# The second norm's gain folded into router, shared and gathered weights in a hybrid decoder layer, and expert pairs released from the shared expert

## The chip, the cores and the metric

The kernel runs on one core of one Trainium2 chip. The metric is the device time of one execution in microseconds. It was run three times; the profiled execution is a further one.

## The reference, cut to what matters

One decoder layer over 512 tokens of width 1024: a mixer (attention and a short convolution), a sandwich of norms, then a mixture of 32 experts with top-1 group and top-2 experts per token, and a shared expert.

```python
h = h + rms_norm(mix, post_mix_norm)
t = rms_norm(h, pre_ffn_norm)                  # x * rsqrt(mean(x*x) + eps) * g   <- g is the gain per feature
logits = t @ w_group_router, t @ w_expert_router
combine = top-1 group, top-2 experts of the group, softmax weights
hid = silu(t @ w_gate[e]) * (t @ w_up[e]) * combine[:, e]
routed = sum over e of hid @ w_down[e]
shared = (silu(t @ w_sh_gate) * (t @ w_sh_up)) @ w_sh_down
h = h + rms_norm(routed + shared, post_ffn_norm)
```

The gain `g` (`pre_ffn_norm`, in the kernel `g_ffn`) is applied per feature. Every use of `t` is a matrix product over features, so the gain can stand in the tokens or in the rows of the weights.

## The kernel before, in words

A Python generator scheduler writes the program out: generators yield conditions, `run` (line 267) picks the one with the lowest priority number that the planner `Progress` (lines 62 to 146) thinks can go on, and its instructions go to the engines' queues in that order. The order of each queue is thus fixed when the program is written; on the chip an engine only waits.

Memory for weights and for large tiles is 25 slots of about 1 MB (`NSLOT`, `slot`, `rel`, `take`, `reserve`, `pump`, lines 181 to 231). `Slots` counts free slots while the program is written. `rel` hands slots back and `pump` at once puts the next queued weight loads on SP's queue, one per free slot; slots asked for with `reserve` go first. Which of the 25 places a tile gets is not decided there: it is given its place when the program's first write to it is reached, and that write waits for the last use of what was there.

The weight loads stand in `Slots.queue` in a fixed order (lines 394 to 406): shared gate and up `(32, 0)` and `(32, 1)`; then 16 pairs of experts, six loads of 1 MB each, named `(expert, part)` with parts 0 and 1 for gate and up and 2 for down: pair 0 is experts 0 and 16, pair 1 is 17 and 1, pair 2 is 2 and 18, pair 3 is 19 and 3; `(32, 2)`, the shared down weight, stands behind pair 2; at the end `gp`, and the rows of `y_d` and `h_d` for the last sum (`kk`, `hb`).

The stages around the change, for four chunks `c` of 128 tokens:

- `out_split_gen` (945) loads the two gains into tile `gb`: `g_mix` in its first half and `g_ffn`, copied to all partitions, in its second.
- `attn_out_gen` (1003) makes the mixer's output; behind its last chunk `take` (1024) hands back six slots and takes `rs` (tables of the router), `xg` (gathered rows) and `hs` (shared hidden values).
- `chain_gen` (1029) does the first norm's sum, stores `h_d`, and makes `t` in tile `x` (`tt(c)`) by one VectorE instruction with the scale per token and the gain (1043).
- `router_gen` (1046) transposes `t` (`ptT`), copies it to `tT`, stores `t_d`, and makes the logits from the router weights `wrt` (in tile `m1`).
- `shared_gen` (1084) makes gate and up of the shared expert in matmuls `psh`, 64 records a chunk, at the lowest priority; after the last chunk and with the routing done (flag `idx`) it sets `gu` and hands back both shared weights and both `tT` tiles (1103).
- `route` (1135) makes the token lists per pair in `rs` on VectorE, ends in `idx`, `wgt`, `cnt`, issues the first two gathers of rows from `t_d`, starts `pairs_gen`, and goes on with `overflow_tables` (1334), which reads and writes `rs` to its last instruction and then hands `rs` back (1283).
- `pairs_gen` (1459) reserves `wk` and `yb`, waits for `gu`, transposes the gathered rows (`xpose`, `pxt`, into `wk`) and then does each pair: gate and up (`pgu`, four steps for part 0, four for part 1), `hidden`, down (`pdn`), a scatter to `y_d`. The two weights of a part are handed back behind it.
- `last_gen` (1549) sums routed and shared parts and writes the output.

Of the kernel before, what the change touches and what calls it, by code (L numbers as in the profile page):

```python
# [18 lines left out]
P = 128  # L19
# [146 lines left out]
def hymba_kernel(ctx: ExitStack, tc: tile.TileContext, xT, xmT, x, meta, cpk, pos, wqkv, wconv, wuq, wukv,  # L166
# [43 lines left out]
    def keep(n):  # L210
        Slots.keep = n
        pump()
# [96 lines left out]
    def every(*needs):  # L309
        return lambda: max(f() for f in needs)  # L310
# [68 lines left out]
    queue_load("conv0", wconv[0], ok=lambda: True)  # L379
    pump()  # L380
    Y.dma_start(mt[:NMETA, :D], meta)
    Y.dma_start(posi, pos)
    for q in range(2):
        Y.dma_start(xs[1][:, q * D:(q + 1) * D], x[(2 + q) * P:(3 + q) * P, :])
# [129 lines left out]
    for k in range(8):  # L514
        mm3(pqm[:NMETA, :160], [xmhl[:, a, k, :] for a in range(2)], [wqk(k, a)[:, 256:416] for a in range(2)],
            k == 0, k == 7)


    ssc = cp.tile([P, NT], F32, name="ssc")
# [391 lines left out]
    def finish(c):  # L911
        ac, pmT, mg = A["ac"], A["m"], A["mg"]
        yield every(at(ac), free_bank(2))
        pb = bank("prb")
        for i in range(4):
            tr(pb[:, i * P:(i + 1) * P], ac[:, i * P:(i + 1) * P])
        S.activation(ac, pb, AF.Copy)
        pb = bank("pmT")
        tr(pb[:, :P], SMs[:, c].rearrange("p h m -> p (h m)"))
        V.tensor_copy(pmT, pb[:, :P])  # L920
        yield at(pmT)
        for i in range(4):
            mm(OUTP[c][:, i * P:(i + 1) * P], vm[:, i * P:(i + 1) * P], pmT, start=False, stop=True,
               skip_group_check=True)
        V.tensor_tensor(ac, OUTP[c], ac, op=OP.mult)
        o = slice(c * 512, (c + 1) * 512)
        S.activation(mg[0][:, o], ac, AF.Copy)
        V.tensor_tensor(mg[1][:, o], ac, mg[0].bitcast(F32)[:, o], op=OP.subtract)
        S.activation(ac, ac, AF.Square)
        V.tensor_reduce(pmT, ac.rearrange("p (i n) -> p n i", i=4), axis=AX.X, op=OP.add)  # L930
        spawn(attn_out_gen(c, [m[:, o] for m in mg]), 4)
        yield every(at(pmT), free_bank())
        ps = bank("pas")
        mm(ps[:, :1], pmT, ones, start=True, stop=True)
        rstd(sst[:, c, 0:1], ps[:, :1], 1.0 / 512)
        cv["fin", c] = True
        if c == NT - 1:
            rel(A["b"])
            Y.dma_start(wrt, wr)


    wo = {}
# [2 lines left out]
    def out_split_gen():  # L945
        for k in (4, 5, 6, 7, 0, 1, 2, 3):
            n = f"out{k // 2}"
            yield every(loaded(n), room(1 if k % 4 else K_WO), idle("ACT", "DVE", early=W_IDLE))
            o = G_AO + k if k < 4 else G_CO + k - 4
            wo[k] = split_half(Slots.have[n], k % 2, "wo", ck[:, o:o + 1])  # L950
            if k % 2:
                rel(got(n))
        yield room(2)
        late["gb"], late["x0"] = slot("gb"), slot("x0")
        Y.dma_start(late["gb"][:, :D], g_mix[None, :].to_broadcast([P, D]))
        Y.dma_start(late["gb"][:, D:2 * D], g_ffn[None, :].to_broadcast([P, D]))
        for c in range(2):
            Y.dma_start(tt(c), x[c * P:(c + 1) * P, :])
        yield room(1)
        late["x1"] = slot("x1")  # L960
        for c in range(2, NT):
            Y.dma_start(tt(c), x[c * P:(c + 1) * P, :])
        keep(0)

    def mix(c):
        return mixs[c // 2][:, (c % 2) * D:(c % 2 + 1) * D]
# [36 lines left out]
    def attn_out_gen(c, mg):  # L1003
        yield every(flag(wo, *range(4)), flag(cv, ("co", c)), flag(late, f"x{c // 2}"))
        if c:
            yield flag(cv, ("done", c - 1))
        yield at(*mg, *(wo[k] for k in range(4)))
        ss = small([P, 4], "ss", bufs=4)
        m = mix(c)
        for half in range(2):  # L1010
            yield free_bank()
            ps = bank("pao")
            for k in range(4):
                mm3(ps, [mg[a][:, k * P:(k + 1) * P] for a in range(2)],
                    [wo[k][:, b * 1024 + half * 512:b * 1024 + (half + 1) * 512] for b in range(2)], k == 0, k == 3)
                yield
            yield flag(cv, ("fin", c))
            o = slice(half * 512, (half + 1) * 512)
            V.scalar_tensor_tensor(m[:, o], ps, sst[:, c, 0:1], m[:, o], op0=OP.mult, op1=OP.add)
            S.activation(junk[:, :512], m[:, o], AF.Square, accum_out=ss[:, half:half + 1])  # L1020
            (V if c + half >= G_POOL else G).tensor_tensor(m[:, o], m[:, o], late["gb"][:, o], op=OP.mult)
        cv["done", c] = True
        if c == NT - 1:
            rt["rs"], rt["xg"], sh["hs"] = take(["rs", "xg", "hs"], *(wo[k] for k in range(4)), *A["mg"])
            rt["place"] = rt["rs"][:, 1792:1920]
            S.activation(rt["place"], slotc, AF.Copy)
        spawn(chain_gen(c, ss), 0 if c == NT - 1 else 1)

    def chain_gen(c, ss):
        gb, m = late["gb"], mix(c)  # L1030
        yield at(ss)
        V.tensor_tensor(ss[:, 2:3], ss[:, 0:1], ss[:, 1:2], op=OP.add)
        rstd(sst[:, c, 1:2], ss[:, 2:3], 1.0 / D)
        yield at(sst[:, c, 1:2], m)
        V.scalar_tensor_tensor(m, m, sst[:, c, 1:2], tt(c), op0=OP.mult, op1=OP.add)
        S.activation(junk, m, AF.Square, accum_out=ss[:, 3:4])
        S.dma_start(h_d[c * P:(c + 1) * P, :], m)
        yield at(ss[:, 3:4])
        rstd(sst[:, c, 2:3], ss[:, 3:4], 1.0 / D)
        if c == NT - 1:  # L1040
            G.memset(rt["xg"], 0.0)
        yield at(sst[:, c, 2:3])
        V.scalar_tensor_tensor(tt(c), m, sst[:, c, 2:3], gb[:, D:2 * D], op0=OP.mult, op1=OP.mult)
        spawn(router_gen(c), 0 if c == NT - 1 else P_ROUTER)

    def router_gen(c):
# [10 lines left out]
        if "lg" not in rt:  # L1057
            yield free_bank()
            rt["lg"] = bank("plg")
            held.append(rt["lg"])  # L1060
        yield every(at(*(tT(k, c * P, (c + 1) * P) for k in (0, 4))), free_bank())
        ps = bank("plT")
        for k in range(0, 8, 2):
            for q in range(2):
# [16 lines left out]
    def acc(c):  # L1081
        return sh["out"][c // 2][:, (c % 2) * D:(c % 2 + 1) * D]

    def shared_gen():
        yield loaded((NE, 0), (NE, 1))
        w = [got((NE, i)) for i in range(2)]
        for c in range(NT):
            yield flag(cv, ("tT", c))
            yield every(at(*w, *(tT(k, c * P, (c + 1) * P) for k in (0, 4))), free_bank(2))
            ps = bank("psh")  # L1090
            for g in range(4):
                for k in range(8):
                    o = (k % 4) * 512 + (g % 2) * 256 + (g // 2) * P
                    mm(ps[:, g * P:(g + 1) * P], w[k // 4][:, o:o + P], tT(k, c * P, (c + 1) * P),
                       start=(k == 0), stop=(k == 7))
                    yield
            yield flag(sh, "hs")
            hs_ = sh["hs"]
            S.activation(hs_[:, c * 512:(c + 1) * 512], ps, AF.Copy)
        yield flag(cv, *(("lg", c) for c in range(NT)))  # L1100
        yield flag(rt, "idx")
        sh["gu"] = True
        rel(*w, *tTs)
        yield flag(sh, "silu")
        hs = hs_[:, :2048].rearrange("p (c f g n) -> p c f g n", c=NT, f=2, g=2)
# [184 lines left out]
                             bounds_check=SEQ - 1, oob_is_err=False)  # L1290

    def xpose(src, dst, by=S):
        for q in range(2):
            ps = bank("pxt")
            for k in range(4):
                tr(ps[:, k * P:(k + 1) * P], src[:, (4 * q + k) * P:(4 * q + k + 1) * P])
            if q and by is V:
                V.tensor_copy(dst[:, q * 512:(q + 1) * 512], ps)
            else:
                S.activation(dst[:, q * 512:(q + 1) * 512], ps, AF.Copy)  # L1300

    def hidden(ps, w, sg, hd):
        S.activation(sg, ps[:, :256], AF.Silu)
# [153 lines left out]
            Y.dma_start(out[c * P:(c + 1) * P, :], h)  # L1457

    def pairs_gen():
        box = reserve("wk", "yb")  # L1460
        ys = None
        yield flag(sh, "gu")
        yield lambda: 0.0 if box else INF
        wk_, yb = box
        rt["wk"] = wk_
        rt["jk"] = wk_.bitcast(BF)[:, 3584:3584 + 512]
        xt_ = wk_[:, :D]
        sg, hd, ht = (wk_[:, D + q * 256:D + (q + 1) * 256] for q in range(3))
# [4 lines left out]
        for j, es in enumerate(pairs):  # L1473
            ps = None
            for i in range(2):
                yield every(loaded(*((e, i) for e in es)), free_bank())
                w = [got((e, i)) for e in es]
                yield at(*w, xt_)
                if ps is None:
                    ps = bank("pgu")  # L1480
                for k in range(4):
                    col2(ps, xt_[:, (4 * i + k) * P:(4 * i + k + 1) * P],
                         [w[q][:, k * 512:(k + 1) * 512] for q in range(2)], i + k == 0, i + k == 4)
                rel(*w)
            hidden(ps, wgt[:, j:j + 1], sg, hd)
            sh["silu"] = True
            if j == S_GO:
# [134 lines left out]
    spawn(conv_gen(), 6)  # L1622
    spawn(conv_out_gen(), 3)
    spawn(route(), P_ROUTE)
    spawn(shared_gen(), 8)
    run()
    overflow()
# [81 lines left out]
```

## Time and profile before

| | us |
|---|---|
| median of 3 runs | 508.37 |
| lowest, highest | 507.75, 508.88 |
| profiled execution, its own time | 507.05 |
| span from the first to the last instruction | 505.3 |
| TensorE busy | 479.0 (95%) |
| VectorE, ScalarE, GpSimd busy | 227.0, 163.4, 87.3 |
| moved by DMA | 151.30 MB, mean 299 GB/s |

All positions are microseconds from the span's start; 1.75 us lie outside of the span. The engines are named PE (TensorE), DVE (VectorE), ACT (ScalarE), POOL (GpSimd) and SP (the queue that issues most transfers). A busy PE is not PE at its peak, since the shares are averages over stages with different limits, and matmul ends are modelled.

### The profile page before, as it was taken

The numbers are of one execution on the slowest core, as the hardware profiler recorded it, in microseconds if no ns is written. First come the engines' busy times: TensorE is split into PE (matmuls) and PEld (weight loads), VectorE is DVE, ScalarE is ACT, GpSimd is POOL, SyncE is SP. The second block draws the span as 40 slices with busy tenths as digits, with TensorE's granted clock in tenths as the row PEclk, the third lists the DMA queues.
The fourth block names the chain that finished last, engine by engine and source line by source line (L and its number), as shares of the span: only waits on it lengthen the run. The fifth ranks groups of instructions, "written<-read, shape, count | busy, mean of one in ns | idle before, by whom it ended". The sixth has DMA issues, their size and how long they took to land. (4 is left out here: it accounts for less than half of the span.)

```text
span 505.3 us, 7279 instructions
## 1 busy us (share of the span) xinstructions
PE 479.0 (95%) x2780; PEld 303.0 (60%) x2780; DVE 227.0 (45%) x522; ACT 163.4 (32%) x334; POOL 87.3 (17%) x114
## 2 busy tenths in 40 slices
PE   8999999999999999997999999999999999988893
PEld 7998999788767788897963333433333333223251
DVE  6478789656877642678832111001111111111175
ACT  5775526445345642532122112211111111111131
POOL 2034234400000002460101111001111111100011
PEclk9999999999999999999999999999999999999997
DMA  8962240090207598399659999999999999999993
GB/s 291 401 248 83 84 167 0 35 382 2 84 2 279 220 354 325 134 382 381 242 239 421 417 423 420 422 416 421 420 420 419 420 420 417 420 419 424 405 365 150
DMA packets 30309, 151.30 MB, mean 299 GB/s; under 512 B 5480, under 2 KB 5864, under 8 KB 16192
## 3 DMA queue, kind: packets, MB, share of 16 engines
q1 hardware_dynamic: 24512, 138.43, 68.1%
q0 software_dynamic: 4464, 8.17, 4.4%
q10 hardware_dynamic: 1296, 4.21, 2.1%
q8 instruction: 23, 0.38, 0.3%
q14 instruction: 14, 0.11, 0.1%
HBM read 140.54 MB, written 18.35 MB: 314 GB/s over the span
## 5 line engine op out<-in xcount | busy, mean ns | idle before, releaser
L314 PE MATMUL pc<-xh,cw 128*128 128x256 f32 (+2 forms) x320 | 70.0, 309 | 0.0
L159 DVE SCALAR_TENSOR_TENSOR wk<-wk,wgt,pgu 128x256 f32<-128x256 f32 x16 | 7.7, 480 | 115.3 <-ACT wk L159 115.3
L314 PEld LDWEIGHTS pc<-xh,cw 128*128 128x128 f32 x320 | 52.3, 189 | 4.0 <-issue 1.3
L159 ACT ACTIVATE wk<-pgu 128x256 f32<-128x256 f32 x16 | 6.1, 383 | 133.7 <-PE pgu L314 133.7
L314 PE MATMUL pc<-xl,cw 128*128 128x256 f32 (+2 forms) x160 | 48.8, 305 | 0.0
L159 DVE COPY yb<-pdn 128x512 f32<-128x512 f32 x15 | 10.4, 692 | 60.4 <-PE pdn L314 60.4
L159 POOL DMA_INDIRECT xg<-t_d,idx x16 | 16.5, 1030 | 114.3 <-PE pxt L314 68.8
L159 POOL DMA_INDIRECT y_d<-yb,sidx x15 | 15.1, 1005 | 93.2 <-DVE yb L159 81.9
L314 PEld LDWEIGHTS pc<-xl,cw 128*128 128x128 f32 x160 | 30.4, 190 | 1.2
L159 ACT ACTIVATE att<-pS,nm 128x128 f32<-128x128 f32 (+3 forms) x32 | 16.9, 527 | 29.3 <-DVE nm L159 27.2
L314 PE MATMUL pS<-kT,qT 128*128 128x128 f32 (+3 forms) x64 | 22.7, 440 | 0.0
L159 POOL TENSOR_TENSOR sst<-rst,neghalf 128x1 f32<-128x1 f32 x12 | 7.5, 633 | 81.5 <-DVE rst L159 78.1
L314 PEld LDWEIGHTS pxt<-ident,xg 128*128 128x128 f32 x128 | 14.0, 140 | 11.3 <-issue 9.7
L314 PE MATMUL pco<-wo,cvh 128*128 128x512 f32 x64 | 20.6, 403 | 0.0
L314 PE MATMUL pao<-wo,mgh 128*128 128x512 f32 x64 | 20.0, 393 | 0.0
L159 POOL TENSOR_TENSOR cw<-ld conv,cw 128x1024 fp32r<-128x1024 f32 x6 | 15.7, 2618 | 18.5 <-ACT cw L159 18.5
L159 ACT ACTIVATE yb<-pdn 128x512 f32<-128x512 f32 x15 | 9.0, 597 | 29.2 <-PE pdn L314 29.2
L314 PE MATMUL psh<-tT,ld (32, 1)_1946 128*128 128x128 f32 x128 | 18.0, 279 | 0.0
L314 PE MATMUL psh<-tT,ld (32, 0)_1944 128*128 128x128 f32 x128 | 17.8, 279 | 0.0
L314 PE MATMUL pxt<-ident,xg 128*128 128x128 f32 x128 | 17.3, 278 | 0.0
L159 DVE TENSOR_REDUCE nm<-pS 128x1 f32<-128x128 f32 (+3 forms) x32 | 15.5, 484 | 1.7 <-PE pS L314 1.4
L314 PEld LDWEIGHTS psh<-tT,ld (32, 1)_1946 128*128 128x128 f32 x128 | 15.9, 192 | 0.2 <-issue 0.2
(486 smaller groups left out, 1190.5 us busy)
## 6 DMA issues: line engine op xcount, KB each, us to landing
ld conv<-in_wconv_dram SPq DMA_DIRECT2D x6, 1024.0 KB
ld out<-in_wout_dram SPq DMA_DIRECT2D x4, 1024.0 KB, 4.7
y_d<-sel SPq DMA_DIRECT2D x4, 1024.0 KB
ld kk<-y_d SPq DMA_DIRECT2D x4, 1024.0 KB
xs<-in_x_dram SPq DMA_DIRECT2D x4, 512.0 KB
x<-in_x_dram SPq DMA_DIRECT2D x4, 512.0 KB
h_d<-mix ACTq DMA_DIRECT2D x4, 512.0 KB
t_d<-x ACTq DMA_DIRECT2D x4, 512.0 KB, 10.2
```

The lines of the kernel that those rows point to most:

```text
L159: r = f(*a, **k)
L314: f(o, *ins, **kw)
```

## The change

The gain `g_ffn` is no longer multiplied into `t`. It is loaded as a small tile, transposed once into `gf` (128 x 8: one column per block of 128 features), and multiplied into the router weights (one VectorE instruction), into the shared gate and up weights (eight ScalarE instructions in a new generator of priority 1), and into the gathered rows as they are copied out of PSUM. `t` itself is made by a ScalarE copy with the scale per token. `pairs_gen` no longer waits for `gu`: `wk` is taken with `rs`, `xg` and `hs`, and `yb` is reserved behind the first half of pair 0. `hs` is written early by a small memset.

```diff
+    gfr = mt[:8, 1536:1536 + P]
+    Y.dma_start(gfr, g_ffn.rearrange("(k p) -> k p", k=8))
...
+    gf = cp.tile([P, 8], F32, name="gf")
+    tr(pqm[:, 480:488], gfr, ident[:8, :8])
+    V.tensor_copy(gf, pqm[:, 480:488])
...
@@ out_split_gen
-        Y.dma_start(late["gb"][:, D:2 * D], g_ffn[None, :].to_broadcast([P, D]))
...
         keep(0)
+        yield flag(cv, "wrt")
+        yield at(wrt)
+        w3 = wrt.rearrange("p (k n) -> p k n", k=8)
+        V.tensor_tensor(w3, w3, gf[:, :, None].to_broadcast([P, 8, 64]), op=OP.mult)
+        cv["wrg"] = True
...
@@ attn_out_gen, behind the last chunk
-            rt["rs"], rt["xg"], sh["hs"] = take(["rs", "xg", "hs"], *(wo[k] for k in range(4)), *A["mg"])
+            rt["rs"], rt["xg"], rt["wk"], sh["hs"] = take(["rs", "xg", "wk", "hs"],
+                                                          *(wo[k] for k in range(4)), *A["mg"])
+            G.memset(sh["hs"][:, 0:1], 0.0)
...
@@ chain_gen
-        V.scalar_tensor_tensor(tt(c), m, sst[:, c, 2:3], gb[:, D:2 * D], op0=OP.mult, op1=OP.mult)
+        S.activation(tt(c), m, AF.Copy, scale=sst[:, c, 2:3])
...
@@ router_gen
-        yield every(at(*(tT(k, c * P, (c + 1) * P) for k in (0, 4))), free_bank())
+        yield every(flag(cv, "wrg"), at(*(tT(k, c * P, (c + 1) * P) for k in (0, 4))), free_bank())
...
-    def shared_gen():
+    def shared_scale_gen():
         yield loaded((NE, 0), (NE, 1))
         w = [got((NE, i)) for i in range(2)]
+        for k in range(8):
+            yield every(at(w[k // 4]), idle("ACT", early=1.0))
+            o = w[k // 4][:, (k % 4) * 512:(k % 4 + 1) * 512]
+            S.activation(o, o, AF.Copy, scale=gf[:, k:k + 1])
+        sh["w"] = w
+
+    def shared_gen():
+        yield flag(sh, "w")
+        w = sh["w"]
...
         yield flag(cv, *(("lg", c) for c in range(NT)))
-        yield flag(rt, "idx")
-        sh["gu"] = True
         rel(*w, *tTs)
...
@@ xpose
-            if q and by is V:
-                V.tensor_copy(dst[:, q * 512:(q + 1) * 512], ps)
+            if by is V:
+                V.tensor_tensor(dst[:, q * 512:(q + 1) * 512].rearrange("p (k n) -> p k n", k=4),
+                                ps.rearrange("p (k n) -> p k n", k=4),
+                                gf[:, 4 * q:4 * q + 4, None].to_broadcast([P, 4, P]), op=OP.mult)
             else:
-                S.activation(dst[:, q * 512:(q + 1) * 512], ps, AF.Copy)
+                for k in range(4):
+                    S.activation(dst[:, q * 512 + k * P:q * 512 + (k + 1) * P], ps[:, k * P:(k + 1) * P], AF.Copy,
+                                 scale=gf[:, 4 * q + k:4 * q + k + 1])
...
@@ pairs_gen
-        box = reserve("wk", "yb")
-        ys = None
-        yield flag(sh, "gu")
-        yield lambda: 0.0 if box else INF
-        wk_, yb = box
-        rt["wk"] = wk_
+        wk_, yb, ys, box = rt["wk"], None, None, None
...
+                if j + i == 0:
+                    box = reserve("yb")
                 rel(*w)
+            if j == 0:
+                yield lambda: 0.0 if box else INF
+                yb = box[0]
...
+    spawn(shared_scale_gen(), 1)
```

## Rows read from the trace of the kernel before

**Rows 1.** The page's second part: GB/s in 40 equal slices of 12.6 us.

```profile
GB/s 291 401 248 83 84 167 0 35 382 2 84 2 279 220 354 325 134 382 381 242 239 421 417 423 420 422 416 421 420 420 419 420 420 417 420 419 424 405 365 150
```

**Rows 2.** Stretches: us, busy of PE, PEld, DVE, ACT, POOL, clock, DMA share, GB/s.

```profile
160.00:210.00 50.00, 50.00 (x286) 39.55 (x285) 24.55 (x42) 22.63 (x43) 9.57 (x10) 1.00 0.69 269
...
246.00:257.00 11.00, 10.94 (x110) 10.77 (x110) 9.73 (x44) 0.60 (x1) 1.58 (x2) 1.00 0.22 61
257.00:262.00 5.00, 4.69 (x29) 2.38 (x30) 0.89 (x6) 2.87 (x4) 0.99 (x1) 1.00 0.84 329
262.00:300.00 38.00, 35.75 (x176) 13.15 (x174) 6.88 (x11) 6.81 (x14) 6.07 (x6) 1.00 1.01 419
300.00:340.00 40.00, 40.00 (x166) 15.43 (x163) 3.73 (x7) 8.28 (x16) 4.05 (x4) 1.00 1.02 420
340.00:470.00 130.00, 120.80 (x570) 44.96 (x568) 18.64 (x30) 19.72 (x40) 18.15 (x18) 1.00 1.02 420
```

**Rows 3.** Timeline of SP's queue: start us, us, engine line op out<-in.

```profile
237.12 0.44 SPq L159 DMA_DIRECT2D ld (18, 2)_2418<-in_we_dram  x1
256.68 0.33 SPq L159 DMA_DIRECT2D ld (32, 2)_2605<-in_we_dram  x1
...
257.90 0.33 SPq L159 DMA_DIRECT2D ld (3, 0)_2654<-in_we_dram  x1
258.33 0.53 SPq L159 DMA_DIRECT2D ld (19, 1)_2680<-in_we_dram  x1
262.40 0.33 SPq L159 DMA_DIRECT2D ld (3, 1)_2682<-in_we_dram  x1
...
272.13 0.33 SPq L159 DMA_DIRECT2D ld (4, 0)_2733<-in_we_dram  x1
```

**Rows 4.** Waits of SP's queue: waited for, us in total, times, longest.

```profile
SPq L159 <- PE psh L314: 19.0, 1, 19.0
...
SPq L159 <- DVE code L159: 0.3, 1, 0.3
```

**Rows 5.** Timeline of PE around the start of the pairs; brackets: idle before, releaser.

```profile
231.13 1.06 PE L314 MATMUL ptT<-ident,x 128*128 128x128 f32 x8 [2.75 <-DVE rs L159]
...
256.49 1.06 PE L314 MATMUL psh<-tT,ld (32, 1)_1946 128*128 128x128 f32 x8
257.38 1.04 PE L314 MATMUL pxt<-ident,xg 128*128 128x128 f32 x8
258.73 0.64 PE L314 MATMUL pgu<-ld (0, 0)_1948,wk 128*64 128x512 f32 x1 [0.31 <-ACT wk L159]
...
271.51 0.59 PE L314 MATMUL pdn<-ld (0, 2)_1972,wk 128*64 128x512 f32 x1
```

**Rows 6.** Timeline of ACT in the same stretch.

```profile
217.48 0.29 ACT L159 ACTIVATE rs<-m 128x128 f32<-128x128 f32 x1
...
224.31 1.06 ACT L159 ACTIVATE m<-mix 128x1024 bf16<-128x1024 f32 x1 [0.88 <-DVE rst L159]
...
231.10 0.60 ACT L159 ACTIVATE hs<-psh 128x512 f32<-128x512 f32 x1 [5.64 <-DMA t_d<-x]
...
258.07 1.09 ACT L159 ACTIVATE wk<-pxt 128x512 f32<-128x512 f32 x2
```

**Rows 7.** Timeline of DVE in the same stretch.

```profile
229.71 1.28 DVE L159 SCALAR_TENSOR_TENSOR x<-mix,sst,gb 128x1024 f32<-128x1024 f32 x1
...
244.23 0.17 DVE L159 SCALAR_TENSOR_TENSOR idx<-ptb,rs 128x16 int32<-128x16 f32 x1
...
257.65 0.17 DVE L159 TENSOR_TENSOR code<-code,rs 128x8 f32<-128x8 f32 x1
```

**Rows 8.** Timeline of POOL: the first gather.

```profile
245.29 1.29 POOL L159 DMA_INDIRECT xg<-t_d,idx  x1 [17.92 <-DVE rs L159]
```

**Rows 9.** Instructions of tile xg: time from issue to landing of its gathers.

```profile
DMA to landing us min/median/max: 7.9/8.1/9.3
```

**Rows 10.** Transfers from 244 to 252 us: GB/s in 40 slices of 0.2 us.

```profile
GB/s 369 532 369 369 492 328 451 287 246 82 0 82 82 0 41 41 143 246 123 205 287 225 164 205 143 246 144 185 184 246 144 123 41 0 0 0 0 0 0 0
```

More of the change, by code (lines that the diff above doesn't have):

```diff
@@ L939, in finish @@
             Y.dma_start(wrt, wr)
+            cv["wrt"] = True
     wo = {}
@@ L1029, in chain_gen @@
     def chain_gen(c, ss):
-        gb, m = late["gb"], mix(c)
+        m = mix(c)
         yield at(ss)
```

## The prediction

> **What bounds the kernel now.** I read the page's slices first. From slice 21 on, that is from 265 us, DMA moves about 420 GB/s without a break until the last 25 us [rows 1]. PE is shown busy nearly all the time as well, but the stretches tell which of the two is short: from 340 to 470 us PE idles 9.2 of 130 us while DMA stays at 420 GB/s, and from 262 to 340 DMA is as full while PE catches up [rows 2]. So from 258 us on the kernel streams weights, and its end stands where the stream's start and its holes put it. A microsecond in which DMA idles before 258 us costs one at the end; a microsecond of PE does not, unless it makes such a hole.
>
> The hole that the change can touch is the stretch from 246 to 257 us: 61 GB/s [rows 2]. SP's queue shows why: load (18, 2), the last of pair 2, is issued at 237.12, the next one, (32, 2), at 256.68 [rows 3], after a wait of 19.0 us for the shared matmuls psh [rows 4]. All 25 slots are full then: rs, xg, hs, two tT, two shared weights and 18 loads, pairs 0 to 2. At 256.49 to 257.55 PE ends psh, then transposes for pair 0 and starts its gate and up at 258.73 [rows 5]. Four loads go out from 256.68 to 258.33 [rows 3]. From 257 to 262 us 329 GB/s pass, 1.65 MB, which is 3.9 us at 420, so the stream stands as if it had started at 258.1, 1.4 us behind the first issue [rows 2, 3].
>
> **How memory is handed out.** Three rows show that a tile's place is fixed at its first write, and waits for what last used it there. hs is taken with the slots of the mixer's weights (line 1024), but its first ScalarE write idles 5.64 us for a store t_d<-x, a reader of a token tile [rows 6]. Load (3, 0) waits 0.3 us for the VectorE tile code [rows 4] and is issued at 257.90; the last instruction that reads rs for code starts at 257.65 and takes 0.17 [rows 3, 7]: it lies where rs lay. Load (19, 1) goes out at 258.33, before any weight of pair 0 is done, though five slots came back and wk and yb had reserved two of them [rows 3]: a reservation holds no memory.
>
> **The change, part by part.**
>
> *The wait of the pairs.* Without the flag, pair 0 can start when its rows are gathered and wk has a place. wk is now taken at line 1024, one load fewer is counted there, but wk is first written by the copies of pair 0. The hand-back of rs (line 1283) comes in the program before that: route goes on at once, while the planner lets a gather land 1.2 + 1.5 + 0.9 + 2.0 us after its issue (lines 135 to 139). So (18, 2) is queued by rs's hand-back, finds the spare place free, and the same 18 loads are in before the hole. wk then gets the place of rs, which is free when overflow_tables is done. My main step is this: **the pairs wait for the router's tables instead of for shared.** It needs no new instruction; the copies on ScalarE wait, PE stands behind them in its queue, and the shared matmuls that are left then stand behind PE's wait.
>
> *How much earlier the tables are.* idx is made at 244.23, the last read of rs ends at 257.82, 13.6 us later [rows 7]; this chain is unchanged. What comes earlier is idx. PE waits 2.75 us, to 231.13, for the last chunk's t [rows 5], which VectorE makes at 229.71 in 1.28 us between router instructions [rows 7]; the memset gives hs an early place, so the 5.64 us on ScalarE go too [rows 6]. Both stalls overlap. I take 2.75 us, the one that the chain shows; bounds are 0 (the next release is late by as much) and 5.64. The tables then end at 255.07.
>
> *The ScalarE copy that makes t.* A ScalarE pass over 128 x 1024 takes 1.06 us [rows 6], the VectorE form 1.28 [rows 7]; the move buys 0.2 us and a place outside VectorE's queue, and is in the 2.75. The Trainium skill, ScalarE: Activation LUTs, section Rules for kernel authors, says the opposite of a multiply: use VectorE, up to about three times faster per element in bf16. Taken at that factor, an estimate from that page, the copy would cost some 2.6 us more, the 2.75 would be gone, and the sum below would come to 515.3. The rows are float32 and decide.
>
> *Pair 0's copies.* Two of 128 x 512, 1.09 us together [rows 6], become eight of 128 x 128, 0.29 each [rows 6]; PE follows piece by piece, so 0.5 us pass to its first matmul: 255.07 + 0.5 = 255.6. It was 258.73.
>
> *What the stream makes of that.* Before, it did not wait for pair 0: four slots came back from shared. Now its first free slots are pair 0's own. From PE's first matmul to the issue into the first weight's place it is 262.40 - 258.73 = 3.67 us [rows 3, 5], so (32, 2) and (19, 0) go out at 259.3, and the stream starts 1.4 later, at 260.7: **2.6 us later than 258.1.** One more load, (3, 0), follows after the second half; the fourth place goes to yb. Three loads of 1.05 MB at 420 GB/s are 7.5 us, to 268.2. The next two come when pair 0's down is done, (272.13 - 258.73) = 13.4 us behind its start [rows 3, 5]: 269.0, flowing at 270.4. That is a hole of 2.2 us. One gather of 0.31 MB (half of what passes from 247 to 250.6 us [rows 10]) fills 0.7 of it: **1.5 us**, between 0 and 2.2. Behind that a pair's six loads take 15 us of DMA and PE does a pair in 13.4, so the stream stays fed.
>
> *The rest, at no cost.* The shared weights' scaling is eight passes of about 0.6 us, 4.8 us, on ScalarE from 160 to 210 us, where it is busy 22.6 of 50 [rows 2] and PE is fed by other work; without that cover it costs up to 4.8. The router weights' product (128 x 512, about 0.7 us) falls into the same stretch of VectorE, 24.6 of 50 [rows 2]. The gain's small load and its transpose come in the first 30 us; they cost 0 to 0.5 us of PE's order. The load of g_ffn that goes is 0.5 MB, 1.2 us of a DMA that is not full there. In pairs 1 to 15 VectorE makes both halves of a copy; VectorE is busy 18.6 of 130 us [rows 2], and DMA covers it. These edits together: 0, from -1 to +1.
>
> *Sum.* 2.6 + 1.5 = 4.1 us later. The rows are of an execution of 507.05 us (span 505.3), 1.3 below the median of 508.37; on the median it is 508.4 + 4.1 = **512.5**. The kernel would be as fast as before if pair 0 started at 251.5.
>
> **Rivals.**
>
> *A: wk has a place at once, and the pairs start with their rows; faster.* Its place is in the router's last 13.6 us: it decides if a slot other than rs's is free for wk, or rs is. Then the gather sets the start: issued at 245.29 - 2.75 = 242.5 [rows 8]. The first two gathers' data ended at 250.6, 5.3 us behind the issue, with DMA otherwise empty [rows 10]; that gives 247.9, and pair 0 at 249.2 (1.35 from pxt to pgu [rows 5]): 2.3 us under the mark, **506.1**. With the landing of 7.9 to 9.3 us that gathers show in the stream [rows 9] it is 251.8, or 508.7. For it: line 1024 takes wk while six places are free. Against it: nothing writes wk then, and hs shows what that leads to [rows 6].
>
> *B: the lead is larger.* With 5.64 us, pair 0 starts at 252.7 and the time is 509.6; only 6.9 would make it even. So "no change" mostly needs part of A.
>
> *C: shared keeps four slots too long; slower still.* Its two weights and two tT now wait for gaps of PE. From 300 to 340 us PE has no idle time at all [rows 2], with a stream that is just fed. Four loads are 10 us; if they are missing there for long, up to that much is lost: 516 to 522. Against it: the same PE work is done by then, and a pair still frees places faster than DMA fills them.
>
> **How the numbers follow.** About 0.2%, 1 us, is what a measurement of this kernel can tell from no change. The main case has 0.53 and gives 509.6 (B's lead) to 515.3 (no lead); C has 0.1. A has 0.3: two thirds of it below 507.4, the rest near even. 0.07 is for small edits that give or take a microsecond. Faster 0.22, same 0.15, slower 0.63. The range takes in A's low end and the main case's high one: 505.9 to 515.5; the main case's own is 509.6 to 515.3.
>
> **What would show it.** Right: in the timeline of ScalarE the first wk copy idles for VectorE's code or rs; PE idles for several us before pgu of pair 0, which starts near 255.6; SP's wait for psh is replaced by one for pgu that ends near 259; the hole in GB/s lasts to about 260.7, with a dent near 269; hs no longer waits for t_d, and idx is made near 241.5. Wrong: pgu of pair 0 before 251.5, with a wk copy that waits for pxt alone (A); dents in GB/s between 270 and 340 us (C); or idx no earlier than 244, which would mean that the stall of 2.75 us only moved.

## The result and the profile after

The changed kernel takes **526.58 us** (median of 4 runs, 525.95 to 527.36), the kernel before in the same session 508.62: a ratio of 1.0347 (95% interval 1.032 to 1.0373). The forecast was 512.5, within 505.9 to 515.5. The direction was right; the size was far off. The profiled execution spans 525.6 us, against 505.3 before: 20.3 us to account for.

Two places hold all of it, and both show in the page's slices, which answer to [rows 1] (slices of 13.1 us). The clock that was granted to PE falls twice, in the third slice and in the twenty-first. In the twenty-first slice GB/s falls to 25, and the next one, from 276 us, has 338; before, the slice from 265 us on already had 421.

```profile
PEclk9978999999999999999979999999999999999998
DMA  8941124064203877499608999999999999999993
GB/s 303 401 197 62 34 75 154 2 225 176 81 2 122 319 281 297 168 350 405 249 25 338 414 422 420 422 419 422 418 424 418 419 420 421 419 421 422 401 377 132
```

**Before 60 us: VectorE waits for a copy.** The timeline of VectorE of the changed kernel, then that of ScalarE, then that of PE (start, duration, engine, line, operation, tiles, and in brackets the idle time before and what ended it):

```profile
16.74 0.29 DVE L159 TENSOR_TENSOR kvs<-mt,kvs 128x128 fp32r<-128x128 f32 x1
26.20 0.17 DVE L159 COPY gf<-pqm 128x8 f32<-128x8 f32 x1 [9.17 <-PE pqm L314]
26.32 0.07 DVE L159 MEMSET ssx<- 128x16 f32 x1
29.73 1.23 DVE L159 TENSOR_TENSOR cw<-ld conv,cw 128x1024 fp32r<-128x1024 f32 x1 [3.34 <-ACT cw L159]
```

```profile
26.43 1.06 ACT L159 ACTIVATE m<-xs 128x1024 bf16<-128x1024 f32 x1 [11.02 <-DVE ssx L159]
...
28.66 1.04 ACT L159 ACTIVATE cw<-ld conv 128x1024 fp32r<-128x1024 f32 x1
```

```profile
25.94 0.22 PE L314 MATMUL pqm<-ident,mt 8*128 8x8 f32 x1
29.75 0.58 PE L314 MATMUL pc<-xh,cw 128*128 128x256 f32 x1 [3.59 <-ACT cw L159]
...
42.00 0.39 PE L314 MATMUL pc<-xh,cw 128*128 128x258 f32 x1 [2.01 <-DVE ctmp L159]
```

The gain's transpose stands on PE behind all projections and starts at 25.94. Its copy to gf stands on VectorE ahead of the memset of ssx, so VectorE does nothing for 9.17 us. ScalarE's sums of squares wait for ssx, and the split of the first convolution weights is queued behind them. Before, these ran while PE was still projecting; the same three engines then read:

```profile
21.22 1.23 DVE L159 TENSOR_TENSOR cw<-ld conv,cw 128x1024 fp32r<-128x1024 f32 x1 [3.93 <-ACT cw L159]
```

```profile
17.32 1.06 ACT L159 ACTIVATE m<-xs 128x1024 bf16<-128x1024 f32 x1 [1.69 <-DVE ssx L159]
```

```profile
26.05 0.32 PE L314 MATMUL pc<-xh,cw 128*128 128x256 f32 x1
```

The windows of the changed kernel give the price (us, busy time and count of PE, PEld, DVE, ACT, POOL, then the granted clock, DMA share, GB/s):

```profile
20.00:30.00 10.00, 6.41 (x49) 6.05 (x48) 0.46 (x3) 3.54 (x6) 0.00 (x0) 0.95 1.03 420
30.00:40.00 10.00, 9.53 (x56) 8.86 (x56) 5.30 (x9) 9.68 (x28) 1.20 (x1) 0.71 0.24 101
40.00:50.00 10.00, 8.00 (x50) 7.82 (x51) 6.89 (x24) 3.36 (x6) 4.19 (x2) 0.83 0.01 3
```

PE is busy 23.94 of these 30 us (30.00 before): 6.06 us are idle time. In its busy time it lacks 5, 29 and 17% of its clock, 0.3 + 2.8 + 1.4 = 4.5 us. Together that is 10.5 us, and that is by how much the load of g_mix is late: 161.45, before 150.97. The split into idle time and clock is read from the windows alone; no run separates the two here.

**From 230 us on: the mechanism that was forecast, with other numbers.** The timelines of VectorE, ScalarE and PE, and SP's queue, which answer to [rows 3, 5, 6, 7]:

```profile
255.09 0.17 DVE L159 SCALAR_TENSOR_TENSOR idx<-ptb,rs 128x16 int32<-128x16 f32 x1
...
268.51 0.17 DVE L159 TENSOR_TENSOR code<-code,rs 128x8 f32<-128x8 f32 x1
```

```profile
238.21 1.15 ACT L159 ACTIVATE x<-mix,sst 128x1024 f32<-128x1024 f32 x1 [2.46 <-POOL sst L159]
...
268.79 2.17 ACT L159 ACTIVATE wk<-pxt,gf 128x128 f32<-128x128 f32 x8 [9.65 <-DVE code L159]
```

```profile
269.21 1.12 PE L314 MATMUL pgu<-ld (0, 0)_1951,wk 128*64 128x512 f32 x1 [4.40 <-ACT wk L159]
...
270.12 1.06 PE L314 MATMUL pgu<-ld (0, 0)_1951,wk 128*64 128x512 f32 x1
...
275.00 0.59 PE L314 MATMUL pgu<-ld (0, 0)_1951,wk 128*64 128x512 f32 x1
```

```profile
250.44 0.42 SPq L159 DMA_DIRECT2D ld (18, 2)_2628<-in_we_dram  x1
275.62 0.33 SPq L159 DMA_DIRECT2D ld (32, 2)_2681<-in_we_dram  x1
...
279.06 0.33 SPq L159 DMA_DIRECT2D ld (3, 0)_2693<-in_we_dram  x1
285.22 0.33 SPq L159 DMA_DIRECT2D ld (19, 1)_2734<-in_we_dram  x1
```

wk lies where rs lay: its first copies wait 9.65 us for the end of the tables, and PE behind them. pgu of pair 0 starts at 269.21, which is 258.73 and the 10.5 us from the front: the pairs start no earlier at all. Then SP issues (32, 2), 6.41 us behind pgu. The windows, answering to [rows 2]:

```profile
267.50:272.00 4.50, 2.79 (x8) 0.94 (x10) 1.21 (x8) 3.19 (x9) 0.00 (x0) 0.55 0.00 1
272.00:275.50 3.50, 3.50 (x14) 0.99 (x12) 0.00 (x0) 0.26 (x1) 0.00 (x0) 0.61 0.00 0
275.50:280.00 4.50, 4.50 (x27) 1.95 (x24) 0.48 (x2) 0.39 (x1) 0.00 (x0) 1.00 0.72 271
280.00:285.00 5.00, 5.00 (x31) 2.62 (x31) 1.20 (x3) 0.98 (x2) 0.99 (x1) 1.00 0.99 418
285.00:290.00 5.00, 5.00 (x26) 1.72 (x24) 0.69 (x1) 0.00 (x0) 1.01 (x1) 1.00 0.88 293
```

After its 4.40 us without work PE is granted 0.55 and 0.61 of its clock, mostly the lower of its two levels (1.2 of 2.4 GHz), and a matmul of pair 0 takes 1.06 us instead of 0.59. The last window is the forecast dent: 293 instead of 420 GB/s over 5 us, 1.5 us. From 300 us on DMA moves 420 GB/s as before.

So the theory that the experiments were to test was this: 8 to 10 us come from the place of one copy, the rest from pair 0, which starts no earlier, at half the clock, and feeds the stream from its own places.

### The profile page after: what moved, and what is told of

Its sections match the earlier page's. It is cut to its first block, busy times and chain, and to the rows that moved or that the text cites. A ratio compares the mean times of both kernels' runs of the same rounds, so it can differ in the third digit from the quotient of the medians.

```text
span 525.6 us, 7292 instructions
## 1 busy us (share of the span) xinstructions
PE 488.8 (93%) x2781; PEld 307.5 (58%) x2781; DVE 231.1 (44%) x536; ACT 165.2 (31%) x337; POOL 83.1 (16%) x114
## 5 line engine op out<-in xcount | busy, mean ns | idle before, releaser
L314 PE MATMUL pc<-xh,cw 128*128 128x256 f32 (+2 forms) x320 | 73.9, 320 | 6.1 <-ACT cw L159 3.6
L314 PEld LDWEIGHTS pc<-xh,cw 128*128 128x128 f32 x320 | 55.4, 201 | 10.7 <-ACT cw L159 3.7
L314 PE MATMUL pc<-xl,cw 128*128 128x256 f32 (+2 forms) x160 | 50.6, 316 | 0.0
L314 PEld LDWEIGHTS pc<-xl,cw 128*128 128x128 f32 x160 | 32.2, 201 | 1.2
L159 DVE TENSOR_TENSOR wk<-pxt,gf 128x512 f32<-128x512 f32 x30 | 19.2, 683 | 10.0 <-PE pxt L314 10.0
L314 PE MATMUL psh<-tT,ld (32, 0)_1947 128*128 128x128 f32 x128 | 18.4, 280 | 0.0
L314 PE MATMUL psh<-tT,ld (32, 1)_1949 128*128 128x128 f32 x128 | 18.4, 278 | 0.0
L314 PEld LDWEIGHTS psh<-tT,ld (32, 1)_1949 128*128 128x128 f32 x128 | 16.1, 192 | 0.2 <-issue 0.2
## 6 DMA issues: line engine op xcount, KB each, us to landing
xs<-in_x_dram SPq DMA_DIRECT2D x4, 512.0 KB, 8.8
x<-in_x_dram SPq DMA_DIRECT2D x4, 512.0 KB
h_d<-mix ACTq DMA_DIRECT2D x4, 512.0 KB
t_d<-x ACTq DMA_DIRECT2D x4, 512.0 KB, 7.3
```

The costliest lines, as they stand in the source:

```text
L159: r = f(*a, **k)
L314: f(o, *ins, **kw)
```

## The experiments

All times are medians; the kernel before, run beside each, was at 508.1 to 509.2. Every kernel from e1 on contains the edit of e1, except e2.

| run | what | us | ratio to before (95%) |
|---|---|---|---|
| after | the change | 526.58 | 1.0347 (1.0320 to 1.0373) |
| e1 | gain's copy later | 518.38 | 1.0190 (1.0161 to 1.0219) |
| e2 | before, with the gain's copy alone | 516.98 | 1.0172 (1.0138 to 1.0205) |
| e4 | e1, PE kept busy 8.2 us | 520.30 | 1.0232 (1.0202 to 1.0263) |
| e8 | e1, PE kept busy 4.2 us | 517.01 | 1.0156 (1.0138 to 1.0173) |
| e3 | e1, wk with a place of its own | 513.42 | 1.0097 (1.0066 to 1.0128) |
| e5 | e1, last x ahead of the router | 517.43 | 1.0162 (1.0141 to 1.0183) |
| e10 | e5, PE's order as well | 517.43 | 1.0181 (1.0151 to 1.0211) |
| e11 | e10 and e8 | 516.14 | 1.0157 (1.0123 to 1.0191) |
| e13 | e10, shared held back | 515.67 | 1.0135 (1.0094 to 1.0175) |
| e12 | e13 and e8 | 514.24 | 1.0114 (1.0073 to 1.0154) |
| e7 | e1, pairs wait for shared | 509.81 | 1.0011 (1.0001 to 1.0021) |
| e9 | e7, last x ahead of the router | 508.05 | 0.9985 (0.9971 to 0.9998) |

**e1: the copy moved.**

```
-    gf = cp.tile([P, 8], F32, name="gf")
-    tr(pqm[:, 480:488], gfr, ident[:8, :8])
-    V.tensor_copy(gf, pqm[:, 480:488])
...
     conv_split(1)
+    gf = cp.tile([P, 8], F32, name="gf")
+    tr(pqm[:, 480:488], gfr, ident[:8, :8])
+    V.tensor_copy(gf, pqm[:, 480:488])
```

> The changed kernel, with the gain's transpose and its copy to gf moved behind the second split of the convolution weights; nothing else. My theory: 10.5 us of the loss arise before 60 us, because the copy to gf stands on VectorE ahead of the memset of ssx and waits there for PE to come through all its projections (it idles 9.17 us, to 26.20; in the kernel before, the memset ran at 17.22). Behind it ScalarE idles 11.02 us, PE 3.59 and 2.01 us, and the granted clock falls to 0.71. With the copy moved those waits go, the load of g_mix is back near 151 us (161.45 in the changed kernel), and the time is 526.6 - 10.5 = 516.1 (515.0 to 517.5). Rival: the gain's own load, its transpose and the longer hold of mt cost the time wherever they stand; then the time stays at 524 or more.

518.38, 8.2 us less; the range asked for 515.0 to 517.5, so the theory holds for four fifths of its 10.5. VectorE's timeline of e1 has the memset at 17.38 (before 17.22), and the copy waits for nothing; the lines of PE and of SP's queue are from the start of the pairs.

```profile
17.38 0.07 DVE L159 MEMSET ssx<- 128x16 f32 x1
...
28.05 0.16 DVE L159 COPY gf<-pqm 128x8 f32<-128x8 f32 x1
```

```profile
260.87 1.11 PE L314 MATMUL pgu<-ld (0, 0)_1951,wk 128*64 128x512 f32 x1 [4.40 <-ACT wk L159]
```

```profile
266.93 0.33 SPq L159 DMA_DIRECT2D ld (32, 2)_2681<-in_we_dram  x1
```

From 20 to 50 us the clock is 1.00, and PE idles 0.9 us. The load of g_mix goes out at 152.95, 8.5 us earlier, but not near 151 as expected; where the other 2.0 us stay is not shown. pgu of pair 0 is at 260.87 instead of 269.21, 8.3 us earlier, and still 2.1 us later than before; the last mix is 0.9 us late (223.86, before 222.94), the rest arises in the router (below).

**e2: the same instructions, alone, in the kernel before.**

```
+    gfr = mt[:8, 1536:1536 + P]
+    Y.dma_start(gfr, g_ffn.rearrange("(k p) -> k p", k=8))
...
+    gf = cp.tile([P, 8], F32, name="gf")
+    tr(pqm[:, 480:488], gfr, ident[:8, :8])
+    V.tensor_copy(gf, pqm[:, 480:488])
```

> The kernel before, with nothing added but the gain's load into mt, its transpose and its copy to gf, at the places where the changed kernel has them; nobody reads gf. My theory: the whole early loss comes with these three instructions, so the time is 508.6 + 10.5 = 519.1 (518 to 520.5), with VectorE's copy idle near 9 us and the clock near 0.7 between 30 and 40 us. Rival: the early loss needs other parts of the change (other orders of loads or of splits that the planner makes of it); then it stays within 1 us of 508.6.

516.98: 7.8 us slower than the kernel before, a microsecond under the range, and the copy reads as it does in the changed kernel. The clock fell less than expected, to 0.83 from 30 to 40 us, and was 1.00 behind that; PE idled 7.0 us between 20 and 50. Three instructions that move 4 KB make some 8 of the 18 us of the loss; put elsewhere (e1) or put in alone (e2), they are worth the same.

```profile
26.57 0.17 DVE L159 COPY gf<-pqm 128x8 f32<-128x8 f32 x1 [9.08 <-PE pqm L314]
26.69 0.07 DVE L159 MEMSET ssx<- 128x16 f32 x1
```

**e4 and e8: the clock.** PE is given work in its wait; the bank is overwritten by the first real matmul.

```
                 if ps is None:
                     ps = bank("pgu")
+                    for q in range(36 if j == 0 else 0):     # e8: 18
+                        T.matmul(ps[:, :P], ident, ident, start=True, stop=True)
```

> As e1, and PE is kept at work in its wait for pair 0's rows: 36 matmuls of 128 x 128 float32, of the kind and speed of psh (8 in 0.9 us, so 4.0 us in all), write into the bank of pgu before its first real matmul overwrites it. In the changed kernel PE idles 4.40 us there, the granted clock reads 0.55 to 0.61 from 267.5 to 275.5, and the first half of pair 0 takes 6.2 us instead of 3.5. My theory: that clock costs 2.7 us, so the time is 2.7 us under that of e1: 513.4 (512.8 to 514.2). Rival: the stream's start does not hang on PE's speed there, or the clock falls for another reason; then it is the same as e1 within 0.7 us.

520.30, which is 1.9 us more than e1 and outside both ranges: my sizing was wrong. A float32 matmul of this kind counts twice in the rows (x72 for 36), so the 36 took 8.21 us and pushed pgu to 264.44. Behind them the clock read 1.00. So e8 took half.

> As e4_fill with 18 matmuls instead of 36. In e4_fill the 36 took 8.21 us (each counts twice), not 4.0, so they ended 3.6 us after pair 0 could have started; yet behind them the clock read 1.00 and the first half of pair 0 took 3.5 us instead of the 5.9 of e1_gain_later. My theory: 18 of them take 4.1 us and end within the wait, pgu starts at 260.9 as in e1_gain_later, its first half takes 3.5 us, and the time is 2.4 us under e1_gain_later's 518.4: 516.0 (515.2 to 516.7). Rival: the stream's start does not hang on the clock: 518.4 within 0.7.

517.01, 1.4 us less than e1: outside both ranges, and less than the 2.4 expected. PE's timeline of e8 and SP's queue of e8:

```profile
256.39 4.18 PE L1502 MATMUL pgu<-ident 128*128 128x128 f32 x36
260.97 0.64 PE L314 MATMUL pgu<-ld (0, 0)_1951,wk 128*64 128x512 f32 x1 [0.39 <-ACT wk L159]
```

```profile
264.64 0.33 SPq L159 DMA_DIRECT2D ld (32, 2)_2699<-in_we_dram  x1
```

From pgu to the first issue it is 264.64 - 260.97 = 3.67 us, to the digit what the prediction took from the kernel before [rows 3, 5]; in e1 it is 266.93 - 260.87 = 6.06. The issue is 2.3 us earlier, the span 2.2 (514.5 for 516.7), the medians 1.4. So the lower clock is shown to delay the first issue, by 2.3 us in these two executions. In medians its price is smaller: 1.4 here, 1.3 and 1.4 where the same 18 matmuls are added to e10 (e11) and to e13 (e12). It also differs between executions: behind a wait of 4.4 us the first issue follows pgu by 6.41 us in the changed kernel, 6.06 in e1, 5.37 in e5, 5.30 in e10 and 6.47 in e13, and by 3.7 in e4, e8, e11 and e12, which have the matmuls.

**e3: a place of its own for wk.**

```
             G.memset(sh["hs"][:, 0:1], 0.0)
+            G.memset(rt["wk"][:, 0:1], 0.0)
```

> As e1, and wk gets a place of its own at once: a memset of one column by GpSimd right where it is taken, as hs has one. The pairs then wait for their rows, not for the tables. My theory: pgu of pair 0 starts 5 us earlier than in e1 (near 253.5 instead of 258.7), PE does not idle and the clock stays up; but a place for wk is one load less before the hole: (18, 2) is the one that now lies where rs lay and is issued when the tables end, near 258.4, with the other loads queued behind it. Stream from 259.8 (1.7 us later than before) with one load more to move (2.5 us): 508.6 + 4.2 = 512.8 (511.5 to 514). Rival A of the prediction: the early start of the pairs is what counts, and the time is 506 to 509. Third: the start of pair 0 changes nothing, 516.1.

513.42, within the range of the first theory; the other two fall. pgu starts at 255.84 (2.3 us later than I expected, with shared matmuls still ahead of it on PE), the clock reads 1.00 throughout, and (18, 2) is what now waits for the tables. PE's timeline and SP's queue of e3:

```profile
255.84 0.64 PE L314 MATMUL pgu<-ld (0, 0)_1951,wk 128*64 128x512 f32 x1
```

```profile
243.07 0.38 SPq L159 DMA_DIRECT2D ld (2, 2)_2440<-in_we_dram  x1
259.87 0.33 SPq L159 DMA_DIRECT2D ld (18, 2)_2629<-in_we_dram  x1
```

Pair 0 starts 2.9 us earlier than before the change, and the kernel is still 4 to 5 us slower than before: one place less means one load of 1.05 MB more behind the hole. This is rival A of the prediction with its place paid for.

**e5, e10, e13: where the lead went.** e5 has the router's first group wait for the last token tiles:

```
         for a, b in GROUPS:
             yield flag(cv, *(("lg", q) for q in range(a, b)))
...
+            yield flag(cv, ("x", 2), ("x", 3))
```

> As e1_gain_later, and the router's work on chunks 0 and 1 waits in the program until the token tiles of chunks 2 and 3 are written, so that the last reciprocal root does not stand behind 16 router instructions on VectorE (in e1_gain_later it ran at 229.08, 2.7 us after the sum that it needs was there, and the last x on ScalarE waited 2.47 us for it). This is the lead that the prediction took for the change itself. My theory: x, its transposes, idx (246.75) and the end of the tables (260.5) come 2.5 to 3 us earlier, pair 0 with them, and the time falls by as much: 515.6 (514.8 to 516.3). Rival: PE's queue puts shared matmuls ahead of the transposes wherever they are free, idx does not move by more than 1 us and the time stays at 517.4 to 518.8.

517.43. The last x is earlier (228.74), idx is not (246.69): the rival's mechanism, at the edge of its range. The profiled span is 0.7 us shorter than that of e1 (516.0), and that is again the clock: pgu starts at 260.82, as in e1, but its first matmul still ran at full speed (0.64 us), and (32, 2) went out at 266.19. e10 puts pps behind the last transposes and ptb behind the logits:

```
             if pps is None:
...
+            if b < NT:
+                yield flag(cv, ("tT", 2), ("tT", 3))
             yield at(oh[:, :, c])
...
+            if b < NT:
+                yield flag(cv, ("lg", 2), ("lg", 3))
             yield at(*(ohp[k * NT + q] for k in range(2) for q in range(a, b)))
```

> e5_lead moved x by 1.15 us (228.74 instead of 229.89) and idx by nothing (246.69): on PE the transposes of x still stood behind shared matmuls and behind pps, and the logits plT behind ptb, which need the router's work on chunks 0 and 1. This run is e5_lead with PE's order changed too: pps of the first router group is issued behind the transposes of chunks 2 and 3, its ptb behind their logits. My theory: plT starts near 234.0 instead of 235.6, the second group's router work on VectorE near 236.5 instead of 238.9, and idx, the tables and pair 0 come 2.3 us earlier than in e1_gain_later (pgu near 258.5); time 518.4 - 2.3 = 516.1 (515.3 to 516.9). Rival: idx stays within 1 us of 246.7, because VectorE's own chain decides; time 517 to 518.5.

517.43, idx at 246.01: the rival again by its numbers, though e13 will show that its reason, VectorE's own chain, is not what holds idx here. PE's timeline of e10 shows what stands ahead of the transposes, long after x has ended at 229.4:

```profile
230.60 1.06 PE L314 MATMUL psh<-tT,ld (32, 1)_1949 128*128 128x128 f32 x8
231.50 0.83 PE L314 MATMUL psh<-tT,ld (32, 0)_1947 128*128 128x128 f32 x6
232.17 1.04 PE L314 MATMUL ptT<-ident,x 128*128 128x128 f32 x8
```

e11 adds e8's matmuls to it.

> e10_lead_order with the 18 matmuls of e8_fill_half in PE's wait. With the gain's copy out of the way, the lead there and the clock kept up, this is the course that the prediction had costed; what is left against the kernel before is the later start of the stream from pair 0's own places (5.1 us behind pgu) and the hole behind it. My theory: 1.4 to 2.3 us under e10_lead_order: 514.3 (513.3 to 515.0), that is 5 us over the kernel before, where the prediction's sum was 4.1. Rival: the two do not add up (the wait is shorter and the matmuls run over it): as e10_lead_order within 0.7 us.

516.14, 1.3 us less than e10: neither expectation. The range had counted on the lead that e10 did not have; the clock's part did add up, at the 1.4 of e8 and not at 2.3. e13 therefore holds the shared matmuls back:

```
         for c in range(NT):
-            yield flag(cv, ("tT", c))
+            yield flag(cv, ("tT", c), *((("tT", 2), ("tT", 3)) if c else ()))
```

> In e10_lead_order the last x ended at 229.4, but the transposes started at 232.17 only, behind shared matmuls that PE's queue had ahead of them, and idx (246.01) moved by 0.7 us, not by the 2.3 expected. This run is e10_lead_order with the shared matmuls of chunks 1 to 3 held back until the transposes of chunks 2 and 3 are in PE's queue, so that PE waits for x and not x for PE. My theory: it is PE's queue, and nothing else, that ate the lead: ptT starts near 229.8, idx near 244.0, the tables end near 257.5, and pgu starts near 258.0 instead of 260.9; time 518.4 - 2.7 = 515.7 (514.8 to 516.5). Rival: VectorE's router work on chunks 0 and 1 is the next in line and keeps idx above 245.5: 516.8 to 518.

515.67, as expected. PE's timeline of e13 has ptT right behind x, VectorE's has idx 2.2 us earlier than e1's 246.75:

```profile
230.08 1.91 PE L314 MATMUL ptT<-ident,x 128*128 128x128 f32 x16
```

```profile
244.59 0.17 DVE L159 SCALAR_TENSOR_TENSOR idx<-ptb,rs 128x16 int32<-128x16 f32 x1
```

So PE's queue held idx back in the changed kernel. But even with the queue cleared, idx only comes back to where it was before the change (244.23). VectorE's waits between its last mix and idx say why, first before the change, then in e13:

```profile
234.40 0.35 DVE L159 TENSOR_SCALAR m<-plT,brt 128x128 f32<-128x128 f32 x1 [0.26 <-PE plT L314]
235.27 0.35 DVE L159 TENSOR_SCALAR m<-plT,brt 128x128 f32<-128x128 f32 x1 [0.52 <-PE plT L314]
...
244.02 0.17 DVE L159 TENSOR_SCALAR rs<-ptb 128x16 f32<-128x16 f32 x1 [0.28 <-PE ptb L314]
```

```profile
226.88 0.15 DVE L159 TENSOR_SCALAR rst<-ss 128x1 f32<-128x1 f32 x1 [1.21 <-ACT m L159]
...
234.63 0.35 DVE L159 TENSOR_SCALAR m<-plT,brt 128x128 f32<-128x128 f32 x1 [0.33 <-PE plT L314]
235.51 0.35 DVE L159 TENSOR_SCALAR m<-plT,brt 128x128 f32<-128x128 f32 x1 [0.52 <-PE plT L314]
...
244.38 0.17 DVE L159 TENSOR_SCALAR rs<-ptb 128x16 f32<-128x16 f32 x1 [0.28 <-PE ptb L314]
```

Before the change VectorE waited 1.06 us in all between the last mix (222.94) and idx, 21.3 us later; the rest of that time it worked. So most of PE's 2.75 us was not on the way to idx. In e13 the two last products x are gone from VectorE's queue, 1.2 us each, but with e5's order a wait of 1.21 us for ScalarE has come in: from the last mix (224.33) to idx it is 20.3 us. That is a lead of 1.0 us, and the last mix being 1.4 us later uses it up.

**e12: both terms put right.** e13 with the 18 matmuls.

> e13_lead_held with the 18 matmuls in PE's wait for pair 0's copies. My theory: both terms that the prediction had wrong behind 230 us, the lead and the clock, are put right here, so only its own two terms are left against the kernel before (2.6 for the stream's later start and 1.5 for the hole) and the 0.9 us by which the last mix still is late: 508.6 + 5.0 = 513.6 (512.8 to 514.5). Rival: as in e11_lead_order_fill the gains do not add up, and it stays at 515 or more.

514.24, within the range. pgu starts at 258.4, 0.3 us before its place before the change, the clock reads 1.00, (32, 2) goes out at 262.11, and from 270 to 280 us 353 instead of 420 GB/s pass, 1.6 us. That the time fell within the range is in part luck. My 2.6 supposes a pair 0 that starts 3.1 us earlier than before; it starts 0.3 earlier, so the stream's start is 5.7 - 0.3 = 5.4 us later (5.1 from pgu to the stream, and the 0.6 by which the stream of before was ahead of pgu). With the hole that is 7.0; the span is 6.7 longer (512.0 for 505.3), the medians 5.6.

**e7 and e9: the pairs wait for shared.** e7 undoes the change of pairs_gen and of the flag gu, and no longer takes wk early or yb behind the first half:

```
+        yield flag(rt, "idx")
+        sh["gu"] = True
         rel(*w, *tTs)
...
-        wk_, yb, ys, box = rt["wk"], None, None, None
+        box = reserve("wk", "yb")
+        ys = None
+        yield flag(sh, "gu")
+        yield lambda: 0.0 if box else INF
+        wk_, yb = box
+        rt["wk"] = wk_
...
```

> As e1_gain_later, but the pairs wait for shared again as in the kernel before: wk and yb are reserved behind it, wk is not taken early. What is left of the change is the gain in the weights and in the copies, x by ScalarE and the early place of hs. My theory: the rest of the loss (518.4 - 509.0 = 9.4 us) is all in the pairs' new wait, so the time is 508.5 (507 to 509.5): the shared weights' scaling, the router weights' product and the eight small copies cost nothing, and PE's idle time between 210 and 246 us is 1.9 us less than before, which the 0.9 us by which the last mix is late take half of. Rival: the scaled copies or the scaling cost some microseconds in the pairs; then 511 or more.

509.81, 0.3 us above the range, and 1.0011 (1.0001 to 1.0021) of the kernel before: the rest of the loss is the pairs' new wait, and what is left of the change (the folded gain, x on ScalarE, the early place of hs) costs about half a microsecond. The folded gain hides even though its parts are longer than forecast (next section). e9 adds e5's line:

> e7_wait_shared with the edit of e5_lead. My theory: pair 0 starts when PE has done the shared matmuls, and not when the router is done; the lead only fills PE's last idle time, 0 to 0.9 us: 508.0 (506.5 to 509.0), not slower than e7_wait_shared and perhaps under the kernel before. Rival: the router decides there too, and the time falls by 2.5 us to 506.

508.05, 0.9985 (0.9971 to 0.9998) of the kernel before: as expected, and the only version that is not slower than it. The gain of 0.15% is less than the 0.2% that a measurement of this kernel can tell from no change.

## Why the prediction was wrong

In spans of the two profiled executions, by the prediction's own terms:

| term | forecast | after | shown by |
|---|---|---|---|
| gain's load, transpose, copy | 0 to 0.5 | 8.3 | e1, e2 |
| pair 0's start besides that | -3.1 | +2.1 | rows; e5, e10, e13 |
| from pair 0's start to the stream, against before | 5.7 | 5.7 | rows of e8, e12 |
| clock in pair 0's first half | none | 2.7 | rows; e8 (2.4 in e1) |
| hole behind the first three loads | 1.5 | 1.5 | windows |
| scalings, product, small copies | 0 | 0 to 0.5 | e7 |
| sum | 4.1 | 20.3 | span |

5.7 is 3.67 + 1.4 (the prediction's, from issue to flow) and the 0.6 us by which the stream of before was ahead of pgu; 6.41 - 3.67 = 2.7. The medians lie 18.0 us apart and not 20.3. In medians, the clock's part is 1.3 to 1.4 (e8, e11, e12), and what the changed kernel would still lose without the early copy, the router's delay and the clock is 5.6 (e12); no run splits these 5.6 further.

- **The step that failed most** is "The gain's small load and its transpose come in the first 30 us; they cost 0 to 0.5 us of PE's order". I costed the transpose on PE, where it takes 0.22 us, and never asked what is queued behind its copy on VectorE. The instruction behind it was ready 9 us earlier, and two other engines hung on that one. That is the question that a wait added to a queue calls for, and the cover that I named was PE's. Against the 0 to 0.5 of the forecast stand 8.3 us.
- **The second is "I take 2.75 us, the one that the chain shows".** In e1 idx is made at 246.75, 2.5 us later than before and not 2.75 earlier; the bounds were 0 and 5.64. The stall moved, as the text said it might: the last x left VectorE's queue and then waited 2.47 us for a root whose input stands in that same queue behind the router; PE, with nothing to wait for, had been given shared matmuls ahead of the transposes. I bounded the lead by the stalls that the rows show, and not by what the queues would hold in their place. The stall that I took was PE's, while idx is made on VectorE, which waited only 1.06 us in that stretch before the change.
- **The clock was missing from the sum.** I forecast that PE idles several microseconds ahead of pair 0, and costed the pair at the speed of a PE that had not idled.
- **Right:** wk in rs's place and the pairs behind the tables; 13.6 us from idx to the last read of rs (268.68 - 255.09 = 13.6); SP's wait for psh replaced by one for pgu; 3.67 us to the first issue; the dent of 1.5 us; hs without its wait; no dents after 300 us, so rival C did not come. Rival A was tried in e3: its early start is real, and it costs a load.
- **The rest at no cost** holds, by cover and not by size: the eight passes over the shared weights took 0.71 us each, not 0.6, and the router weights' product 1.79 us, not 0.7; e7 shows both hidden.
- **The ScalarE copy that makes t** takes 1.13 to 1.15 us in e1, the VectorE form 1.28 [rows 7]; the copy's own speed played no part in the loss. The rule of the Trainium skill, ScalarE: Activation LUTs, section Rules for kernel authors, to use VectorE for a multiply, was weighed in the prediction; its figure is for bf16, and for this float32 row it is not borne out.

## What to carry to other kernels

A small instruction costs what stands behind it in its engine's queue: find the cross-engine wait that it adds, the first instruction behind it, and who waits for that, and put it where its input is already there. A gap that you forecast on PE has a second price, the clock of what follows. A wait taken away gives nothing where the same place, or the same queue, holds the next one; ask what will be put in the gap.

## What the runs showed of the hardware

The clock's two falls were not expected. Behind 3.59 us without work ahead of the convolution PE was granted 0.71 of the clock from 30 to 40 us; behind the same 3.59 us in e2 it was 0.83. Behind 4.40 us ahead of pair 0 it was 0.55 and 0.61 over eight microseconds, and in e5 and e10, behind as long a wait, less of pair 0's first half was slow (see e8). In e8 the same wait filled with 4.18 us of matmuls whose results nobody reads gave 1.00, and saved 2.3 us of the issue time. The Trainium skill, TensorE: Matmul & The Clock Gate, section Part 1, says that an idle PE falls to the lower level; the traces agree (0.55 behind the 4.40 us). So the fall was in reach of the prediction.
